# A hybrid mixer and expert layer: expert tables split ahead into fp16 halves in DRAM, three gathered blocks instead of two, 80 early score tiles

## Chip, core and metric

One of the eight cores of a Trainium2 chip runs the whole layer as one program. The metric is the device time of one execution in microseconds (us); less is better. The kernel before takes 4614.6 us (median of three runs, 4611.57 to 4617.51).

## What is computed

1024 latent tokens and 256 context tokens of 1024 features go through a parallel pair of token mixers (HGRN2 and gated linear attention, chunked scans with 12 heads in all), and then through a product-key expert layer (PEER) with 16,384 experts. The second half is what the change is mostly about:

```python
q = (tok @ wq).reshape(-1, PEER_HEADS, 2, PEER_SUB_DIM)      # 8 heads, two halves of 128
s1 = jnp.einsum("nhd,kd->nhk", q[:, :, 0], k1)               # 128 first keys
s2 = jnp.einsum("nhd,kd->nhk", q[:, :, 1], k2)               # 128 second keys
v1, i1 = lax.top_k(s1, 16)
v2, i2 = lax.top_k(s2, 16)
cand = (v1[..., :, None] + v2[..., None, :]).reshape(-1, 8, 256)
top_s, top_c = lax.top_k(cand, 16)
expert = take(i1, top_c // 16) * 128 + take(i2, top_c % 16)  # 128 experts per token
gate = jax.nn.softmax(top_s, axis=-1)
act = jax.nn.gelu(jnp.einsum("pd,ped->pe", xb, jnp.take(u, eb, axis=0)))
out = jnp.einsum("pe,ped->pd", gb * act, jnp.take(v, eb, axis=0))
```

The tables u and v have 16,384 rows of 1024 float32 numbers each (67 MB each).

## The kernel before

The work stands in four stages, one behind the other, each an `ExitStack` of pools in `tile_layer`.

**Heads.** For each head, 128-column slabs of the input projection are loaded (SP's DMA queue), split into two fp16 halves (`split`, L90: ScalarE makes the high half, VectorE the low half) and multiplied with the normalised tokens. Every product of two split operands is three matmuls (`mm3`, L95). `proj` (L299) makes one 128-column product for one range of tokens (24 matmuls), `v_natural` (L335) the value columns. Gates, scans, states and outputs of a head are computed while TensorE makes the projections of the next.

**Merge.** Merge gates, output projection, norm of the second sub-layer (`next_norm`, with `h2_rows`, which writes the normalised rows of the gathered tokens to DRAM), and the key choice of the first 512 tokens (`choosing`).

**Product keys and early scores.** `route` turns the top-16 lists of 128 tokens into key numbers and gates; `gate_block` makes the gate matrix of 32 tokens: one-hot rows `oh` on VectorE, matmuls `pgm` of a one-hot with a gated one-hot on TensorE, an eviction `gs` on ScalarE, and a store to `G_d`. Meanwhile `early_tile` makes scores of 128 experts for all tokens that go through every expert: `u_load`, `u_turn` (TensorE transposes `put`, two ScalarE copies, a GpSimd subtraction), `u_act` (matmuls `ph`, Gelu) and a store to `act_d`. How many early tiles stand between the steps of `prep` is set by a table of made-up durations that `prep` yields, against `U_US`.

**Groups of experts.** 32 groups of four expert tiles. Each tile's scores are either read back (`acr`) or made there (`ph`), multiplied by gates (`weigh`), and multiplied by the value rows (`v_tile`, `out_unit`, matmuls `pe`), whose sums VectorE adds to `acc`.

Blocks of 128 tokens come in two sorts. The first `NGB` = 2 blocks do not go through every expert: for each of their 128 slots GpSimd gathers one row of u per token by an indirect DMA, VectorE forms the dot product, and later one row of v per token is gathered and added to `gacc` (`gathering`, L864): 256 gathers of 512 KB per block. The others go through all 128 expert tiles. `gathers` puts two gathers behind every early tile, once both blocks are routed; `feed` spreads the rest over the groups in proportion to TensorE's work.

The program order of each engine and DMA queue is made by a scheduler at build time from the order in which the code records instructions; at run time each engine and each queue goes through its own list in order, and waits on semaphores.

## Time and profile before

| | |
|---|---|
| median of three runs | 4614.6 us (4611.57 to 4617.51) |
| span of the profiled execution | 4615.8 us |
| TensorE busy | 4416.1 us (96%) |
| VectorE busy | 2794.3 us (61%) |
| ScalarE busy | 1519.0 us (33%) |
| GpSimd busy | 1459.2 us (32%) |
| bytes moved by DMA | 709.58 MB, mean 154 GB/s |
| mean granted TensorE clock | 0.969 |

The profile is of one execution. Its span runs from the first to the last instruction, and it lies inside the spread of the three runs, so span and run time are taken as one number here. What one execution adds ahead of its first and behind its last instruction does not show in it. PE is TensorE (PEld its weight loads), DVE VectorE, ACT ScalarE, POOL GpSimd, SP the engine that issues most loads. A busy share is a mean over the four stages, which differ.

### The profile page before, as it was taken

The page shows a single profiled execution, that of the slowest core. Times are in us where ns is not written, and L with a number is a line of the kernel's source. Part 1 is how long each engine was busy: PE and PEld are TensorE (multiplying, and loading weights), DVE is VectorE, ACT ScalarE, POOL GpSimd, SP SyncE. Part 2 cuts the span into 40 slices and gives each one's busy share as a digit, 9 for nine tenths or more (in the row PEclk, how much of TensorE's full clock was granted, in tenths as well). Part 3 has the DMA queues.
Part 4 walks back from the last instruction along what each step waited for, and adds up shares of the span by engine and source line. Part 5 has one row for each costly group of instructions (what it writes and reads, how often), then busy time and mean ns, then how long its engine had stood idle before and what let it go on. Part 6 is the DMA issues. An engine that isn't in the chain of part 4 may idle for free.

```text
span 4615.8 us, 61540 instructions
## 1 busy us (share of the span) xinstructions
PE 4416.1 (96%) x24821; PEld 2509.4 (54%) x24821; DVE 2794.3 (61%) x4946; ACT 1519.0 (33%) x2251; POOL 1459.2 (32%) x1077
## 2 busy tenths in 40 slices
PE   7999999999999989899989999999999999999998
PEld 3666566566554444455555555555555555455554
DVE  5434544334564486656985443677777776877777
ACT  6333432322332222343334433322222222222222
POOL 2111111100110345523543111444444444444442
PEclk9999999999999999799998988999999999999999
DMA  4111111101147532224433435767777776777775
GB/s 165 37 33 38 42 38 33 46 27 43 42 121 231 193 117 78 84 100 148 137 130 131 149 140 178 235 230 264 253 255 251 236 253 230 256 252 258 246 248 199
DMA packets 421019, 709.58 MB, mean 154 GB/s; under 512 B 22031, under 2 KB 286714, under 8 KB 416638
## 3 DMA queue, kind: packets, MB, share of 16 engines
q1 hardware_dynamic: 219812, 291.35, 19.4%
q0 software_dynamic: 73728, 268.47, 17.7%
q10 hardware_dynamic: 127194, 145.83, 9.3%
q8 instruction: 195, 3.19, 0.3%
q14 instruction: 90, 0.74, 0.1%
HBM read 610.14 MB, written 95.43 MB: 153 GB/s over the span
## 4 chain that ended last, share of the span: by engine, by line
PE 71%; DVE 12%; ACT 6%; DMA 4%; issue 4%; POOL 3%; ACTq 0%; SPq 0%; DVEq 0%; POOLq 0%
PE pe L99 16%; PE ph L99 15%; PE pgm L1010 8%; ACT gs L1012 3%; PE pj_f0h L99 2%; PE pv_h L99 2%; PE pv_g L99 2%; PE pj_f1h L99 2%; PE pj_m L99 2%; PE pj_qh L99 2%; PE put L913 2%; PE pj_gh L99 1%; PE pq L99 1%; PE pso L99 1%; PE pj_kg L99 1%
## 5 line engine op out<-in xcount | busy, mean ns | idle before, releaser
L99 PE MATMUL ph<-hb,uT 128*128 128x256 f16 (+1 forms) x6144 | 1094.7, 335 | 5.1 <-ACT ac L933 2.6
L99 PE MATMUL pe<-v,w 128*128 128x512 f16 x4608 | 1013.0, 380 | 18.9 <-DVE acc L1102 13.3
L99 PEld LDWEIGHTS <-uT 128*128 128x128 f16 x6144 | 619.3, 101 | 409.4 <-issue 34.1
L99 PEld LDWEIGHTS <-w 128*128 128x128 f16 x4608 | 451.2, 98 | 567.3 <-issue 20.0
L920 POOL TENSOR_TENSOR uT<-uf,uT 128x512 f16<-128x512 f32 x256 | 361.0, 1420 | 476.1 <-ACT uf L919 474.2
L892 POOL DMA_INDIRECT row_False<-in_peer_u_dram,idx x256 | 303.2, 1185 | 459.1 <-DVE row_False L871 410.2
L892 POOL DMA_INDIRECT row_True<-in_peer_v_dram,idx x256 | 296.7, 1159 | 452.1 <-DVE gacc L876 406.3
L871 DVE SCALAR_TENSOR_TENSOR row_False<-row_False,h2n 128x1024 f32<-128x1024 f32 x256 | 345.0, 1354 | 139.0 <-DMA row_False<-in_peer_u_dram,idx 139.0
L1010 PE MATMUL pgm<-oh 128*128 128x128 f16 x1536 | 391.2, 410 | 37.9 <-ACT gs L1012 31.2
L876 DVE SCALAR_TENSOR_TENSOR gacc<-row_True,dots,gacc 128x1024 f32<-128x1024 f32 x254 | 356.2, 1402 | 1.6
L88 DVE TENSOR_TENSOR oh<-iota,rTr 128x1024 f16<-128x1024 f16 x192 | 151.8, 827 | 325.8 <-PE pgm L1010 325.8
L1012 ACT ACTIVATE gs<-pgm 128x512 f32<-128x512 f32 x192 | 204.8, 1067 | 419.0 <-PE pgm L1010 418.9
L1010 PEld LDWEIGHTS <-oh 128*128 128x128 f16 x1536 | 223.5, 146 | 179.0 <-issue 64.2
L933 ACT ACTIVATE ac<-ph 128x256 f32<-128x256 f32 (+1 forms) x256 | 125.3, 494 | 441.2 <-PE ph L99 434.1
L1102 DVE TENSOR_TENSOR acc<-pe,acc 128x512 f32<-128x512 f32 x372 | 252.9, 686 | 15.1 <-PE pe L99 15.0
L92 ACT ACTIVATE v<-vn 128x1024 f16<-128x1024 f32 x128 | 135.0, 1057 | 337.9 <-DMA vn<-in_peer_v_dram 222.5
L917 ACT ACTIVATE uT<-put 128x512 f16<-128x512 f32 x256 | 153.5, 600 | 272.3 <-PE put L913 264.2
L93 DVE SCALAR_TENSOR_TENSOR v<-vn,v 128x1024 f16<-128x1024 f32 x128 | 177.2, 1392 | 72.9 <-ACT v L92 68.5
L99 PE MATMUL pj_m<-hb,w_m 128*128 128x512 f16 x768 | 186.1, 399 | 2.2 <-DVE lf_g L85 1.6
L99 PE MATMUL pq<-hb,w_wq 128*128 128x512 f16 x768 | 180.7, 384 | 4.5 <-POOL w_wq L88 3.0
L99 PEld LDWEIGHTS <-hb 128*128 128x128 f16 x1536 | 150.3, 98 | 17.3
L919 ACT ACTIVATE uf<-put 128x512 f32<-128x512 f32 x256 | 154.9, 605 | 11.8 <-issue 7.6
(360 smaller groups left out, 5948.0 us busy)
## 6 DMA issues: line engine op xcount, KB each, us to landing
un<-in_peer_u_dram SPq DMA_DIRECT2D x128, 512.0 KB
vn<-in_peer_v_dram SPq DMA_DIRECT2D x128, 512.0 KB
G_d<-gs ACTq DMA_DIRECT2D x24, 2048.0 KB
gt<-G_d ACTq DMA_DIRECT2D x32, 1536.0 KB
act_d<-ac ACTq DMA_DIRECT2D x48, 384.0 KB
acr<-act_d SPq DMA_DIRECT2D x48, 384.0 KB
mw<-in_ada_w_dram SPq DMA_DIRECT2D x32, 512.0 KB
w_wq<-in_peer_wq_dram SPq DMA_DIRECT2D x32, 512.0 KB
```

Of the source, the lines that this page charges most:

```text
L88: eng.tensor_tensor(out=out, in0=in0, in1=in1, op=op)
L93: return V.scalar_tensor_tensor(out=lo, in0=src, scalar=float(scale), in1=hi, op0=ALU.mult, op1=ALU.subtract)
L99: PE.matmul(ps, lhsT=a(k), rhs=b(k), start=n == 0, stop=n == last)
L871: V.scalar_tensor_tensor(out=row, in0=row, scalar=1.0, in1=h2n, op0=ALU.mult, op1=ALU.mult, accum_out=dots[:, s:s + 1])
L876: V.scalar_tensor_tensor(out=gacc[n], in0=row, scalar=dots[:, s:s + 1], in1=gacc[n], op0=ALU.mult, op1=ALU.add)
L892: G.indirect_dma_start(out=row, out_offset=None, in_=src[0], in_offset=bass.IndirectOffsetOnAxis(ap=gsel[n][0][:, s:s + 1], axis=0))
L917: S.activation(hi, pv, AF.Copy, scale=SU)
L919: S.activation(uf, pv, AF.Copy, scale=SU)
L920: pace[0] = G.tensor_tensor(out=lo, in0=uf, in1=hi, op=ALU.subtract)
L1010: PE.matmul(pgm[:, t, :], lhsT=oh[:, 0, :, t1 + t], rhs=oh[:, j, :, t1 + t], start=j == 2, stop=j == 3)
L1012: S.activation(gs[:, :, q0:q0 + 4].rearrange("p i n -> p n i"), pgm, AF.Copy, scale=SA / SG)
L1102: vmark[0] = V.tensor_tensor(out=acc[n][:, hs], in0=ps, in1=acc[n][:, hs], op=ALU.add)
```

## The change

- During the heads, a generator `presplit` goes through both expert tables: 512 pieces of 128 rows x 512 columns are loaded (`pin`), split into fp16 halves (`pout`) and stored to `u_d` and `v_d`. `meanwhile` draws three pieces for each 512-column projection.
- `u_load` then reads the halves of u out of `u_d` by a transposing DMA, two of 256 KB for a tile; the TensorE transposes, the ScalarE copies and GpSimd's subtraction of `u_turn` go. `v_tile` reads ready halves from `v_d`; its split goes.
- The tables' rows are now grouped by first key, so a tile's 128 rows are neighbours, and `gate_block` swaps the roles of the keys.
- Three blocks (0, 1 and 4) are gathered, five go through every expert; `ph` is 256 and 384 columns wide instead of 256 and 512, and a group has 10 units of `pe` instead of 12.
- One-hot rows are made for 4 tokens at once instead of 8, so the token index, which is innermost, puts the 128 elements of a matmul operand 8 bytes apart instead of 16.
- 80 early tiles instead of 48; the made-up durations change, and `prep` routes the gathered blocks first. Row buffers of the gathers: 6 instead of 4; a gather's issue no longer stands behind `pace` (GpSimd's subtraction).

```diff
-TB = 8           # tokens whose one-hot rows are made at once
-NGB = 2          # blocks of 128 tokens whose experts' rows are gathered
-T0 = NGB * P     # the other tokens go through every expert
-TD = T - T0
+TB = 4
+GB = (0, 1, 4)
+DB = (2, 3, 5, 6, 7)
+TD = len(DB) * P
+DH = ((2, 4), (5, 8))
-U_US = 10.5
+U_US = 6.9
-AHEAD = 4
+AHEAD = 6
+PRE = 3.0
...
-    early = [e for e in range(NKEY) if e % GR == 0 or (e % GR == 2 and (e // GR) % 4 < NE2)]
+    early = [e for e in range(NKEY) if e * 5 % 8 < 5]
+    u_d = dram.tile([NKEY, 2, P, D], F16, name="u_d")
+    v_d = dram.tile([NKEY, P, 2, D], F16, name="v_d")
+    u_r = peer_u[0].rearrange("(e p) d -> e p d", p=NKEY)
+    v_r = peer_v[0].rearrange("(e p) d -> e p d", p=NKEY)
...
+        def presplit():
+            jobs = [(w, e, hf) for e in range(NKEY) for w in range(2) for hf in range(2)]
+            ins, outs = [], []
+            def load():
+                w, e, hf = jobs[len(ins)]
+                t = hs_.tile([P, HD], F32, name=f"pin{w}_{e}_{hf}", tag="pin", bufs=3)
+                ld(out=t, in_=(v_r if w else u_r)[e, :, hf * HD:(hf + 1) * HD])
+                ins.append(t)
+            def store():
+                w, e, hf = jobs[len(outs) - 1]
+                cs = slice(hf * HD, (hf + 1) * HD)
+                ld(out=v_d[e][:, :, cs] if w else u_d[e][:, :, cs].rearrange("a p d -> p a d"), in_=outs[-1])
+            load()
+            load()
+            for n, (w, e, hf) in enumerate(jobs):
+                if len(ins) < len(jobs):
+                    load()
+                o = hs_.tile([P, 2, HD], F16, name=f"pout{w}_{e}_{hf}", tag="pout", bufs=3)
+                split(ins[n], o[:, 0], o[:, 1], SV if w else SU)
+                if outs:
+                    store()
+                outs.append(o)
+                yield
+            store()
+        def meanwhile(w):
+            owed_[0] += PRE * w
+            while owed_[0] >= 1.0:
+                owed_[0] -= 1.0
+                next(ahead, None)
...
+            meanwhile(LEN[r] / HT)
...
-        for n in range(NGB):
+        for n in GB:
...
-                    with tc.issue_after(pace[0].ins):
-                        G.indirect_dma_start(out=row, out_offset=None, in_=src[0],
+                    G.indirect_dma_start(out=row, out_offset=None, in_=src[0],
...
-        un = pu.tile([P, D], F32, name=f"un{e}", tag="un", bufs=2)
-        ld(out=un, in_=u_r[:, e, :])
-        return un
+        uT = pu.tile([P, 2, KC, P], F16, name=f"uT{e}", tag="uT", bufs=3)
+        for j in range(2):
+            nc.sync.dma_start_transpose(out=uT[:, j], in_=u_d[e][j])
...
-                oh = pg.tile([P, 4, P, TB], F16, name=f"oh{n}_{c0}", tag="oh", bufs=2)
+                oh = pg.tile([P, 4, P, TB], F16, name=f"oh{n}_{c0}", tag="oh", bufs=4)
-                tt(V, oh[:, 0], iota, col(0), ALU.is_equal)
-                tt(V, oh[:, 1], iota, col(1), ALU.is_equal)
+                tt(V, oh[:, 0], iota, col(1), ALU.is_equal)
+                tt(V, oh[:, 1], iota, col(0), ALU.is_equal)
...
         def prep():
-            sel = route(NGB)
-            yield 9.0
-            yield from gating(range(NGB, 4), sel)
-            for n in range(NGB):
+            for n in (0, 1):
                 route(n)
-                yield 6.0
-            first = []
-            yield from choosing(1, ppg, lambda: first.append(route(4)))
-            yield from gating(range(4, 8), first[0])
+                yield 16.0
+            sel = route(2)
+            yield 16.0
+            yield from gating((2, 3), sel)
+            yield from choosing(1, ppg, lambda: route(4))
+            sel = route(5)
+            yield 16.0
+            yield from gating((5, 6, 7), sel)
...
-        vn = pd.tile([P, D], F32, name=f"vn{e}", tag="vn", bufs=2)
-        ld(out=vn, in_=v_r[:, e, :])
         v16 = pd.tile([P, 2, D], F16, name=f"v16_{e}", tag="v16", bufs=2 * GR)
-        vmark[0] = split(vn, v16[:, 0], v16[:, 1], SV)
+        ld(out=v16, in_=v_d[e])
```

Where instructions move, two places matter below. The first is the heads. This is SP's list of transfers around the loads of head 3 (`w_vh`, `w_gh`, `w_f0h`, `w_f1h` and `w_qh` are weight slabs of 512 KB), before:

```order
L340 DMA w_vh_1731<-in_w_in_dram 128x8x128
L340 DMA w_vh_1735<-in_w_in_dram 128x8x128
L168 DMA w_gh_2120<-in_w_in_dram 128x8x128
L168 DMA w_f0h_2319<-in_w_in_dram 128x8x128
L168 DMA w_f1h_2403<-in_w_in_dram 128x8x128
```

And the same queue in the changed kernel, between one weight slab of a head and the next (`pin` is a piece of a table that is loaded, `pout` its two halves that are stored):

```order
L175 DMA w_qh_3932<-in_w_in_dram 128x8x128
L317 DMA pin_32_1_3476<-in_peer_u_dram 128x512
L323 DMA v_d<-pout_31_0_3472 256x1x512
L317 DMA pin_32_0_3482<-in_peer_v_dram 128x512
L323 DMA v_d<-pout_31_1_3478 256x1x512
L317 DMA pin_32_1_3516<-in_peer_v_dram 128x512
L323 DMA u_d<-pout_32_0_3484 128x2x512
L317 DMA pin_33_0_3522<-in_peer_u_dram 128x512
L323 DMA u_d<-pout_32_1_3518 128x2x512
L317 DMA pin_33_1_3528<-in_peer_u_dram 128x512
L323 DMA v_d<-pout_32_0_3524 256x1x512
L390 DMA w_vh_4027<-in_w_in_dram 128x8x128
```

A weight slab that stood right behind the last one now stands behind some six loads and six stores of pieces (five of each are shown). On ScalarE, between two evictions of the projection `pj_f0h` of one head, before:

```order
L530 ACTIVATE at_f0h_2324<-pj_f0h_1_2351 128x512
L486 ACTIVATE ss_h_2182<-ss_h_2182 128x8
L530 ACTIVATE at_f0h_2324<-pj_f0h_2_2377 128x512
```

And in the changed kernel (`pout` from `pin` is the high half of a piece):

```order
L581 ACTIVATE at_f0h_2962<-pj_f0h_1_2995 128x512
L93 ACTIVATE pout_30_1_3292<-pin_30_1_3252 128x512
L430 ACTIVATE ke_h_1_3378<-lf_h_3311 128x1024
L432 ACTIVATE qe_h_1_3377<-lf_h_3311 128x1024
L536 ACT_TABLE_LOAD
L536 ACTIVATE ss_h_2820<-ss_h_2820,eps 128x8
L93 ACTIVATE pout_31_0_3298<-pin_31_0_3258 128x512
L93 ACTIVATE pout_31_1_3304<-pin_31_1_3290 128x512
L581 ACT_TABLE_LOAD
L581 ACTIVATE at_f0h_2962<-pj_f0h_2_3039 128x512
```

Three pieces now stand between two evictions; the next eviction cannot start before the piece ahead of it has landed. The second place is VectorE in the groups of experts, where `row` instructions use gathered rows and `acc` adds a sum from TensorE, before:

```order
L1102 TENSOR_TENSOR acc_22317<-pe_2_0_28692,acc_22317 128x512
L871 SCALAR_TENSOR_TENSOR row_2_False,dots_28521<-row_2_False,h2n_28519 128x1024
L1102 TENSOR_TENSOR acc_22317<-pe_2_1_28709,acc_22317 128x512
L871 SCALAR_TENSOR_TENSOR row_3_False,dots_28521<-row_3_False,h2n_28519 128x1024
L871 SCALAR_TENSOR_TENSOR row_5_False,dots_28521<-row_5_False,h2n_28519 128x1024
L1102 TENSOR_TENSOR acc_22318<-pe_3_0_28726,acc_22318 128x512
```

And in the changed kernel:

```order
L1142 TENSOR_TENSOR acc_26690<-pe_2_1_29054,acc_26690 128x512
L929 SCALAR_TENSOR_TENSOR row_37_False,dots_28376<-row_37_False,h2n_28374 128x1024
L929 SCALAR_TENSOR_TENSOR row_38_False,dots_28376<-row_38_False,h2n_28374 128x1024
L929 SCALAR_TENSOR_TENSOR row_39_False,dots_28376<-row_39_False,h2n_28374 128x1024
L929 SCALAR_TENSOR_TENSOR row_40_False,dots_28376<-row_40_False,h2n_28374 128x1024
L89 TENSOR_TENSOR acr_29199<-acr_29199,gt_29027 128x640
L89 TENSOR_TENSOR ac_29077<-ac_29077,gt_29027 128x640
L1125 TENSOR_TENSOR w_33_29139<-ac_29077,w_33_29139 128x640
```

More gathered rows stand between two sums, and no split of v. In the built order of the changed kernel 156 of the 768 uses of a gathered row stand ahead of the first `acc` and 612 behind it.

## Rows read from the trace of the kernel before

**Rows 1.** The page's part 1: busy us, share of the span, instructions.
```profile
PE 4416.1 (96%) x24821; PEld 2509.4 (54%) x24821; DVE 2794.3 (61%) x4946; ACT 1519.0 (33%) x2251; POOL 1459.2 (32%) x1077
```

**Rows 2.** Windows by stage: length, busy us by engine, granted clock, DMA share, GB/s.
```profile
70.00:1471.00 1401.00, 1355.80 (x9080) 848.61 (x9080) 637.02 (x1078) 493.87 (x711) 182.27 (x97) 0.98 0.19 55
1471.00:1887.00 416.00, 380.27 (x1768) 179.40 (x1768) 252.29 (x861) 112.93 (x154) 173.94 (x119) 0.96 0.43 137
1887.00:2890.00 1003.00, 942.53 (x4742) 568.81 (x4740) 606.79 (x1498) 395.07 (x566) 327.29 (x233) 0.91 0.38 136
2890.00:4616.00 1726.00, 1693.03 (x9080) 898.46 (x9080) 1272.98 (x1459) 477.73 (x760) 771.07 (x618) 0.99 0.74 244
```

**Rows 3.** The chain that ended last, in order of time: start us, us, what.
```profile
150.30 12.98 PE pj_f1h L99 x72
163.28 10.38 PE pj_qh L99 x48
...
3115.20 7.80 PE ph L99 x48
3123.00 15.54 PE pe L99 x72
```

**Rows 4.** Windows inside the heads: busy us by engine, clock, DMA share, GB/s.
```profile
300.00:1200.00 900.00, 877.94 (x5997) 558.29 (x5997) 377.48 (x661) 322.53 (x466) 117.36 (x60) 0.98 0.14 38
```

**Rows 5.** Windows in the last stage in which the DMA engines were full.
```profile
3085.00:3105.00 20.00, 20.00 (x110) 10.68 (x109) 15.47 (x22) 4.82 (x8) 10.05 (x8) 1.00 0.99 361
3130.00:3150.00 20.00, 20.00 (x110) 10.73 (x109) 15.39 (x20) 6.53 (x10) 10.45 (x8) 1.00 0.98 347
3180.00:3200.00 20.00, 20.00 (x110) 10.67 (x108) 16.77 (x20) 5.99 (x11) 8.84 (x7) 1.00 0.96 342
```

**Rows 6.** Groups by line in 2890 to 4616 us: count, busy us, mean ns, idle before.
```profile
L876 DVE SCALAR_TENSOR_TENSOR gacc<-row_True,dots,gacc 128x1024 f32<-128x1024 f32 x254 | 356.2, 1402 | 1.6
L892 POOL DMA_INDIRECT row_True<-in_peer_v_dram,idx x256 | 296.7, 1159 | 452.1 <-DVE gacc L876 406.3 <-DVE row_False L871 13.8 <-issue 12.1
L892 POOL DMA_INDIRECT row_False<-in_peer_u_dram,idx x202 | 239.5, 1186 | 392.8 <-DVE row_False L871 360.4 <-DVE gacc L876 8.0 <-issue 7.7
L92 ACT ACTIVATE v<-vn 128x1024 f16<-128x1024 f32 x122 | 128.7, 1056 | 329.9 <-DMA vn<-in_peer_v_dram 214.5 <-PE pe L99 106.6 <-PE put L913 8.4
L917 ACT ACTIVATE uT<-put 128x512 f16<-128x512 f32 x160 | 95.5, 597 | 267.6 <-PE put L913 259.5 <-PE pe L99 7.9
```

**Rows 7.** TensorE's timeline, gate matmuls and transposes: start us, us, operation, count.
```profile
2000.65 2.02 PE L1010 MATMUL pgm<-oh 128*128 128x128 f16 x8
2002.50 1.04 PE L99 MATMUL ph<-hb,uT 128*128 128x512 f16 x4
...
2012.47 0.60 PE L913 MATMUL put<-ident,un 128*128 128x128 f32 x4
...
2887.85 1.04 PE L913 MATMUL put<-ident,un 128*128 128x128 f32 x8
```

**Rows 8.** VectorE's timeline in the last stage: start us, us, operation.
```profile
3510.53 1.22 DVE L93 SCALAR_TENSOR_TENSOR v<-vn,v 128x1024 f16<-128x1024 f32 x1
...
3523.00 0.96 DVE L88 TENSOR_TENSOR acr<-acr,gt 128x768 f32<-128x768 f32 x1 [2.43 <-DMA acr<-act_d]
3523.88 0.95 DVE L88 TENSOR_TENSOR ac<-ac,gt 128x768 f32<-128x768 f32 x1
...
3527.80 0.68 DVE L1102 TENSOR_TENSOR acc<-pe,acc 128x512 f32<-128x512 f32 x1
3528.40 1.28 DVE L876 SCALAR_TENSOR_TENSOR gacc<-row_True,dots,gacc 128x1024 f32<-128x1024 f32 x1
3529.59 0.68 DVE L1102 TENSOR_TENSOR acc<-pe,acc 128x512 f32<-128x512 f32 x1
```

126 lines of the change are left out of this document (60 added, 66 removed).

## Prediction

> **What bounds the kernel now.** First the page's busy line: TensorE 96%, every other engine at or under 61% [rows 1]. That is a mean, so next the windows by stage [rows 2]: heads to 1471 us, merge to 1887, product keys with early scores to 2890, groups of experts to the end. TensorE is busy 1356 of 1401, 380 of 416, 943 of 1003 and 1693 of 1726 us. So each stage is TensorE's, and the stage table also shows who is next: in the groups VectorE has 1273 us of work and the DMA engines are 0.74 full at 244 GB/s; in the heads DMA is almost unused (0.19). The change takes from TensorE and gives to DMA and VectorE, so the question in each stage is which of the three ends last afterwards.
>
> The stretches of matmuls that follow each other in the chain give the prices [rows 3]: 48 `ph` matmuls (24 of 256 and 24 of 512 columns, one tile's scores) take 7.80 us, 72 `pe` of 512 columns 15.54, that is 0.216 each; 48 of a projection 10.38, so one `proj` of 512 columns 5.19.
>
> **Groups of experts (1726 us).** *TensorE:* 320 units of 12 `pe` instead of 384: 3840 x 0.216 = 829 us. Live tiles 48 instead of 80, each 640 columns instead of 768: 7.80 x 5/6 = 6.5 us, 312 us. The transposes go. Sum 1141.
>
> *VectorE:* 612 uses of a gathered row stand here in the changed order; now 458, the gathers that the two rows of POOL count [rows 6]. In the timeline an `acc` and a gather's use together take 3527.80 to 3529.59, of which 0.60 are the sum's and 1.19 the use's [rows 8]. 612 x 1.19 = 728; 320 sums x 0.60 = 192; gating and subtraction 0.88 each at 768 columns, so 128 x 2 x 0.88 x 5/6 = 188; the end some 30. Sum about 1140. The mean of 1402 ns in the group is more than 1.19 us [rows 6]; by it the uses cost 858 and the sum is 1270. The splits of v go (1.22 us each [rows 8]).
>
> *DMA:* a gather moves 128 x 1024 x 4 bytes = 0.524 MB. Now 458 x 0.524 + 80 tiles of u and 128 of v x 0.524 + 48 read-backs x 0.393 + 32 gate loads x 1.573 + ends 8 = 427 MB, against 244 x 1726 = 421 in the table [rows 2], so the account holds. After: 612 x 0.524 = 321; v 67; 48 transposing pairs 25; 80 read-backs x 0.328 = 26; 32 gate loads x 1.311 = 42; ends 8. Sum 490 MB in fewer us. In the three windows where DMA was full it moved 361, 347 and 342 GB/s [rows 5]: mean 350, so 490 MB take 1400 us. Bounds: 361 gives 1357; the stage's own 244/0.74 = 330 gives 1485.
>
> So DMA ends last here, ahead of TensorE by some 260 us. VectorE's list is in order, and a use of a row waits for its landing; behind it stand the sums that free `pe`'s PSUM tiles, so TensorE waits as well. With filling and end I take **1420**, a gain of 306. The six row buffers allow 6 x 1420/612 = 14 us between issue and use, enough, since 3.1 MB in flight are 9 us at 350 GB/s.
>
> **Product keys and early scores (1003 us).** TensorE before: 48 tiles x 7.8 = 374; gate matmuls, 8 in 1.85 us (2000.65 to the `ph` at 2002.50), 0.231 each [rows 7], x 1536 = 355; transposes, keys and the rest some 148; 877. So 126 us are gaps and stretches at the lower clock (granted 0.91 [rows 2]). After: 80 x 6.5 = 520; transposes of u gone, some 98 left; 1280 gate matmuls at a new price. A gate matmul has 128 columns and takes longer than a `pe` of 512 (0.216), so something in it costs; what sets it apart is that both operands' elements lie 16 bytes apart. They will lie 8 apart. Bounds: no better, 0.231; as the contiguous 128-column transposes, 0.11 (four `put` end after 0.60 us, eight after 1.04, so four more cost 0.44 [rows 7]). I take 0.12, half of 0.231, in proportion to the bytes that an operand spans, which is also near the contiguous row: 154 us, against 296. Sum 520 + 98 + 154 + the same 126 = **900**, with 1040 if the spacing buys nothing. Gain 103. VectorE, 607 busy now, gets some 100 more uses at 1.19: under 730, hidden below 900. GpSimd loses its subtractions.
>
> [...]
>
> The transposing loads occur nowhere in this trace. As ordinary traffic, a tile's 0.524 MB take 1.5 us at 350 GB/s, against 900/80 = 11 us per tile; two tiles are fetched ahead. I cost them at that; the bad end is a rival. [...]
>
> **Heads (1401 us).** Added: 512 pieces, each 0.262 MB in and 0.262 out: 268 MB. ScalarE: 512 x 0.597 (the 128 x 512 copy [rows 6]) = 306, with 494 now makes 800 of 1401. VectorE: half of 1.22 and a little, 0.65 x 512 = 333, with 637 now makes 970. Neither fills. DMA: three pieces per `proj` are 1.57 MB in 5.19 us, besides 38 GB/s of weights [rows 4], 0.2 MB. At 361 GB/s [rows 5] that is 4.9 us, just hidden; at the rate that the weights' traffic shows per share, 38/0.14 = 271, it is 6.5, and TensorE loses 1.3 us x 171 `proj` = 220. What waits then: ScalarE's list has three pieces between two evictions, the evictions free the two PSUM tiles of the projections; and on SP weight slabs stand behind piece stores that wait for VectorE. Near the good end, since 171 projections are 888 of the 1401 us and no pieces are drawn in the others, where DMA catches up, I take **+60**; ends 0 and 220. A sixth more VectorE work in front of the scans is in it.
>
> **Merge (416 us).** Eight more small transposes and stores beside 380 us of matmuls: 0.
>
> **Sum.** 4615.8 + 60 - 103 - 306 = **4267**. The span of 4615.8 is 1.2 us above the median, so the same number stands for the time. The runs differ by 0.13%; 0.2% is taken as the least that can be told from no change.
>
> **Rivals.**
> 1. *Forecast*, 4140 to 4390: chance 0.60.
> 2. *The heads pay the slow DMA rate*: 220 instead of 60, 4427. For it: the weights' 271 GB/s is the only rate that the heads themselves show [rows 4]; against: 342 to 361 in the groups [rows 5]. 0.11.
> 3. *The spacing buys nothing*: gate matmuls stay at 0.231, 142 us more, 4409. For it: no row shows another spacing; against: the only other 128-column rows are contiguous and twice as fast [rows 7]. 0.11.
> 4. *DMA does not bind in the groups*: at a lasting 420 GB/s the 490 MB take 1170 us; then VectorE and TensorE (1141) set about 1190, and the time is 4037. For it: DMA was never asked for more than in bursts; against: even full it moved 361 at most [rows 5]. 0.08.
> 5. *The transposing loads are slow*, the one that ends above before. TensorE takes one tile of early scores in 6.5 us and cannot start without it. At a tenth of 361 GB/s a tile takes 14.5 us: the keys' stage becomes 80 x 14.5 = 1160, and if the transfer holds the DMA engines in the groups too, these have 48 x 14.5 + (490 - 25)/0.35 = 2025 instead of 1420. Time 5130 (4530 if the engines stay free). It decides from 1.5 + 349/48 = 8.8 us per tile (60 GB/s) on: there the groups alone eat the gain of 349. [...] 0.10.
>
> **How the numbers follow.** The likeliest is case 1, 4267. Cases 2 and 3 widen the range upward to 4490 (both with a bad end of the groups), downward I go to 4090, part of the way to case 4; left out are most of case 4, case 5, together 0.17. Faster: cases 1 to 4 less a remainder, 0.88; slower: case 5 and a little, 0.11; same 0.01.
>
> **What will show it.** Heads: the stage's length, ScalarE's waits for `pin`, DMA share (0.19 + 268 MB/350 GB/s/1401 = 0.74 forecast). Keys: the pitch of eight gate matmuls (0.93 us expected, 1.85 if wrong), waits of `ph` for `uT`. Groups: GB/s near 345 and DMA share near 1 with TensorE at 0.80 busy, waits of VectorE for rows; if instead DMA has room and TensorE is full, case 4. A transposing load that lands after more than 8 us makes the prediction wrong, as would a new wait of SP's queue that holds back weights in the heads.

## The result: slower by 4.4%

| | before | changed | forecast |
|---|---|---|---|
| median of four runs, us | 4616.1 (4611.6 to 4622.3) | 4837.2 (4786.1 to 4869.2) | 4267 (4090 to 4490) |
| ratio, 95% interval | | 1.0437 (1.0383 to 1.0492) | |
| span of the profiled execution | 4615.8 | 4784.2 | |
| heads | 1401 | 1632 (+231) | +60 |
| merge | 416 | 422 (+6) | 0 |
| product keys and early scores | 1003 | 1068 (+65) | -103 |
| groups of experts | 1726 | 1592 (-134) | -306 |

The changed kernel is slower, outside the range, and by another sign than forecast. The stages are cut at the first merge matmul, the first `ph` and the first `pe`, in every kernel below. Their differences, 231 + 6 + 65 - 134 = 168, are the whole difference of the two profiled spans; three terms of the sum are off, by 171, 168 and 172 us. The profiled execution is the quickest of the four; the others took 43 to 83 us more, and no profile says in which stage. The slowest execution, 4869.2 us, is 1.7% above the quickest, counts as a slow run and is left out of the ratio, so differences of medians below go by the median of the other three, 4828.7.

**The profile after.** The page's busy line, which answers to [rows 1]:

```profile
PE 3910.2 (82%) x22778; PEld 2283.1 (48%) x22778; DVE 3095.4 (65%) x5908; ACT 1377.2 (29%) x2098; POOL 1417.7 (30%) x1077
```

TensorE is busy 506 us less, and the kernel takes longer: it now waits. In the chain that ended last, by engine, DMA stands where TensorE stood with 71%:

```profile
DMA 35%; PE 20%; DVE 18%; issue 13%; POOL 6%; ACT 6%; SPq 2%; ACTq 0%; DVEq 0%; POOLq 0%
```

The windows by stage, which answer to [rows 2] (length, busy us of TensorE, its weight loads, VectorE, ScalarE and GpSimd, granted clock, DMA share, GB/s):

```profile
70.00:1702.00 1632.00, 1413.42 (x9080) 877.89 (x9080) 984.36 (x1591) 790.30 (x1224) 183.16 (x97) 0.94 0.70 212
1702.00:2124.00 422.00, 381.56 (x1762) 179.35 (x1763) 249.77 (x848) 115.86 (x162) 173.53 (x118) 0.96 0.44 136
2124.00:3192.00 1068.00, 842.90 (x5786) 605.73 (x5785) 674.16 (x1938) 292.26 (x404) 331.19 (x241) 0.91 0.87 194
3192.00:4784.00 1592.00, 1227.49 (x6000) 606.00 (x5998) 1162.39 (x1482) 139.97 (x248) 725.67 (x612) 0.88 1.06 304
```

Read share and rate together. In the groups the engines of the DMA are full (1.06) at 304 GB/s; before, full windows moved 342 to 361 [rows 5]. In the keys' stage they are 0.87 full at 194 GB/s. Something takes DMA time without moving bytes. TensorE, busy 0.77 of the groups' stage where it was 0.98, is granted a clock of 0.88 there, where it was 0.99.

The waits of the heads (engine, line, for whom; us in total, times, longest):

```profile
DVE pout L94 <- ACT pout L93: 405.2, 309, 4.8
...
ACT pout L93 <- DMA u_d<-pout: 253.5, 174, 14.0
ACT pout L93 <- DMA v_d<-pout: 214.1, 158, 4.4
```

ScalarE stands still for 468 us because a piece's output buffer is still being stored, and VectorE behind it. I had said that waits for `pin`, the loads, would show; it is the stores. In the chain that ended last, landings of `u_d` and `v_d` stores make up 34% of the heads' stage. The waits of TensorE itself (the three longest):

```profile
PE kt_h L443 <- ACT kn_h L438: 49.4, 8, 8.5
PE py_g L644 <- ACT v_g L401: 16.5, 5, 5.4
PE pv_h L100 <- ACT v_h L401: 16.0, 9, 3.3
```

Added up over the heads, TensorE waits 170.5 us for ScalarE (22.8 before), 39.4 for VectorE (22.0) and 7.9 for GpSimd (none). That is 173 us more, and the other 58 of the 231 are TensorE's own: the same 9080 matmuls take 1413.42 us at a granted clock of 0.94, and 1355.80 at 0.98 before [rows 2]. The sign that the prediction named for SP's queue, weight slabs held back behind stores, does not show: waits for weight slabs come to 24 us, 26 before.

In the keys' stage TensorE waits for the transposing loads:

```profile
PEld L100 <- DMA uT<-u_d: 135.4, 21, 14.7
PE ph L100 <- DMA uT<-u_d: 127.7, 20, 14.2
```

and its timeline shows such a wait beside gate matmuls of the new spacing:

```profile
2235.34 0.60 PE L100 MATMUL ph<-hb,uT 128*128 128x256 f16 x2 [4.17 <-DMA uT<-u_d]
2250.19 2.74 PE L100 MATMUL ph<-hb,uT 128*128 128x256 f16 x12 [14.25 <-DMA uT<-u_d]
2252.73 1.13 PE L1052 MATMUL pgm<-oh 128*128 128x128 f16 x8
2253.67 1.16 PE L100 MATMUL ph<-hb,uT 128*128 128x256 f16 x6
```

Eight gate matmuls give way to the next after 2253.67 - 2252.73 = 0.94 us; at twice the spacing it was 1.85 [rows 7]. In the groups TensorE waits for VectorE's sums, and VectorE for gathered rows:

```profile
PE pe L100 <- DVE acc L1142: 292.2, 61, 14.7
...
DVE gacc L934 <- DMA row_True<-in_peer_v_dram,idx: 205.4, 123, 10.5
```

So there are two questions: what the transposing loads cost in the last two stages, and what in the pieces' way through ScalarE's list slows the heads. A scale for small differences: four kernels here have the very same heads (the changed one, e3, e5, e7), and they took 1632, 1636, 1642 and 1635 us. Keys and groups repeat less well where transposing loads are in them: 1031 to 1075 and 1579 to 1648 us in the changed kernel and the runs below that keep the transposing loads and alter the pieces.

### The profile page after: what moved, and what is told of

It is laid out like the page before. It is cut to its first block, busy times and chain, and to the rows that moved or that the text cites. A ratio compares the mean times of both kernels' runs of the same rounds, so it can differ in the third digit from the quotient of the medians.

```text
span 4784.2 us, 61229 instructions
## 1 busy us (share of the span) xinstructions
PE 3910.2 (82%) x22778; PEld 2283.1 (48%) x22778; DVE 3095.4 (65%) x5908; ACT 1377.2 (29%) x2098; POOL 1417.7 (30%) x1077
## 4 chain that ended last, share of the span: by engine, by line
DMA 35%; PE 20%; DVE 18%; issue 13%; POOL 6%; ACT 6%; SPq 2%; ACTq 0%; DVEq 0%; POOLq 0%
DMA row_True<-in_peer_v_dram,idx 10%; DMA u_d<-pout 6%; PE ph L100 6%; DMA v_d<-pout 5%; DMA uT<-u_d 4%; DMA row_False<-in_peer_u_dram,idx 4%; POOL row_False L949 3%; DMA gt<-G_d 3%; PE pgm L1052 3%; DVE pout L94 3%; DVE gacc L934 2%; ACT pout L93 2%; PE pj_m L100 2%; PE pq L100 2%; DVE row_False L929 2%
## 5 line engine op out<-in xcount | busy, mean ns | idle before, releaser
L100 PE MATMUL ph<-hb,uT 128*128 128x256 f16 (+1 forms) x6144 | 908.6, 306 | 134.9 <-DMA uT<-u_d 127.7
L949 POOL DMA_INDIRECT row_False<-in_peer_u_dram,idx x384 | 481.1, 1253 | 688.5 <-DVE row_False L929 579.2
L949 POOL DMA_INDIRECT row_True<-in_peer_v_dram,idx x384 | 444.3, 1157 | 689.7 <-DVE gacc L934 574.1
L94 DVE SCALAR_TENSOR_TENSOR pout<-pin,pout 128x512 f16<-128x512 f32 x512 | 372.0, 734 | 406.3 <-ACT pout L93 405.2
L934 DVE SCALAR_TENSOR_TENSOR gacc<-row_True,dots,gacc 128x1024 f32<-128x1024 f32 x381 | 488.1, 1281 | 213.1 <-DMA row_True<-in_peer_v_dram,idx 205.4
L929 DVE SCALAR_TENSOR_TENSOR row_False<-row_False,h2n 128x1024 f32<-128x1024 f32 x384 | 477.1, 1262 | 155.3 <-DMA row_False<-in_peer_u_dram,idx 149.3
L93 ACT ACTIVATE pout<-pin 128x512 f16<-128x512 f32 x512 | 319.5, 628 | 527.4 <-DMA u_d<-pout 253.5
L89 DVE TENSOR_TENSOR oh<-iota,rTr 128x512 f16<-128x512 f16 x320 | 131.1, 439 | 252.3 <-PE pgm L1052 219.1
L1052 PE MATMUL pgm<-oh 128*128 128x128 f16 x1280 | 178.2, 295 | 52.6 <-ACT gs L1053 28.0
L1052 PEld LDWEIGHTS <-oh 128*128 128x128 f16 x1280 | 146.1, 117 | 77.7 <-issue 56.1
```

The lines of the kernel that those rows point to most:

```text
L89: eng.tensor_tensor(out=out, in0=in0, in1=in1, op=op)
L93: S.activation(hi, src, AF.Copy, scale=float(scale))
L94: return V.scalar_tensor_tensor(out=lo, in0=src, scalar=float(scale), in1=hi, op0=ALU.mult, op1=ALU.subtract)
L100: PE.matmul(ps, lhsT=a(k), rhs=b(k), start=n == 0, stop=n == last)
L929: V.scalar_tensor_tensor(out=row, in0=row, scalar=1.0, in1=h2n, op0=ALU.mult, op1=ALU.mult, accum_out=dots[:, s:s + 1])
L934: V.scalar_tensor_tensor(out=gacc[n], in0=row, scalar=dots[:, s:s + 1], in1=gacc[n], op0=ALU.mult, op1=ALU.add)
```

## Experiments on the last two stages

**Splitting ahead left out (e2).** The other tiles are not split; every tile reads tile 0's halves.

```diff
-            jobs = [(w, e, hf) for e in range(NKEY) for w in range(2) for hf in range(2)]
+            jobs = [(w, e, hf) for e in range(1) for w in range(2) for hf in range(2)]
...
-            nc.sync.dma_start_transpose(out=uT[:, j], in_=u_d[e][j])
+            nc.sync.dma_start_transpose(out=uT[:, j], in_=u_d[0][j])
...
```

> The changed kernel with only the first 4 of the 512 pieces split during the heads; every expert tile then reads tile 0's halves, so the splitting of the other tiles is left out, and nothing else. Theory (the heads pay for the pieces, and nothing of them is left afterwards): the heads' stage goes back from 1632 us to about 1401, keys stay near 1069 and groups near 1599, so the time falls by about 231, to some 4560 to 4610, still about that of the kernel before. Rival (the pieces' stores also disturb what comes later, or the heads were slowed by the re-laid buffers): the heads stay above 1550, or the later stages shrink too.

The four executions took 4607.5, 4539.1, 4637.5 and 4638.0 us, the kernel before beside them 4623.0 (median). The heads' window:

```profile
70.00:1482.00 1412.00, 1355.43 (x9080) 848.43 (x9080) 639.24 (x1082) 495.26 (x714) 181.61 (x96) 0.98 0.19 57
```

1412 us, with the busy times of before to within 3 us: of the heads' loss of 231 us, 220 are the pieces'. Without that loss the rest of the change gains little: the quickest execution is 1.8% below the kernel before, the other three are within 16 us of it.

**TensorE turns u again (e3).** The transposing loads are undone, and with them go a buffer of `uT` (two for three) and one of `ph` (one for two).

```diff
-        for j in range(2):
-            nc.sync.dma_start_transpose(out=uT[:, j], in_=u_d[e][j])
+        un = pu.tile([P, D], F32, name=f"un{e}", tag="un", bufs=2)
+        ld(out=un, in_=u_r[e])
...
+        for q in range(2):
...
+            for k in range(4):
+                PE.transpose(pt[:, k * P:(k + 1) * P], un[:, (q * 4 + k) * P:(q * 4 + k + 1) * P], ident)
...
+            S.activation(hi, pv, AF.Copy, scale=SU)
...
+            S.activation(uf, pv, AF.Copy, scale=SU)
+            G.tensor_tensor(out=lo, in0=uf, in1=hi, op=ALU.subtract)
```

> The changed kernel with the transposing loads alone undone: u is read as plain fp32 rows (the same bytes per tile) and turned by TensorE, split by ScalarE and GpSimd as in the kernel before; splitting in the heads, three gathered blocks, spacing and v's halves stay. Theory A (the transposing loads cost three to four times their bytes in DMA time, 5 to 6.5 us of the 16 engines per tile): keys fall from 1069 to about 950 (80 tiles x 1.1 us of transposes come back to TensorE, the 128 us of waits for uT go), groups from 1599 to about 1400 to 1450, at 340 to 350 GB/s; in all 270 to 300 us less, about 4540. Theory B (the third gathered block fills the DMA engines whatever brings u in): keys gain some 50, groups stay within 40 us of 1599 at 305 GB/s; about 4750.

4559.1 us, ratio to before 0.986 (0.9842 to 0.9878): with this one part undone the change is a small gain, of 1.4%. Keys and groups:

```profile
2127.00:3162.00 1035.00, 900.25 (x6399) 669.22 (x6397) 763.29 (x1929) 455.50 (x737) 540.34 (x404) 0.95 0.57 200
3162.00:4560.00 1398.00, 1228.32 (x6400) 640.15 (x6400) 1235.83 (x1482) 232.45 (x428) 898.85 (x702) 0.95 0.94 346
```

The groups do what theory A says: the same bytes at 346 GB/s, 1398 us. The keys' stage does not (1035, not 950): the waits for `uT` go, but TensorE has 57 us of work more and waits 57.8 us for GpSimd's half of `uT`.

**The third gathered block undone (e5).**

```diff
-GB = (0, 1, 4)
-DB = (2, 3, 5, 6, 7)
+GB = (0, 1)
+DB = (2, 3, 4, 5, 6, 7)
...
-            yield from choosing(1, ppg, lambda: route(4))
-            sel = route(5)
-            yield 16.0
-            yield from gating((5, 6, 7), sel)
+            yield from choosing(1, ppg, lambda: first.append(route(4)))
+            yield from gating((4, 5, 6, 7), first[0])
```

> The changed kernel with the third gathered block alone undone: blocks 0 and 1 gather, block 4 goes through the gate matrix and the expert tiles again (768 columns). Theory A (transposing loads cost more, the third block as such is worth its price): without the block DMA has 134 MB less, but TensorE has 768 `pe` and 256 gate matmuls more: groups about 1500 to 1560 with TensorE above 0.9 busy, keys 1100 to 1140 as each tile is longer; total about 4750 to 4830, little gained. Theory B (the third block is what makes the change slower): groups fall to 1450 or less and the total to below 4700.

4701.3 us, ratio 1.0162 (1.0135 to 1.019). The groups:

```profile
3330.00:4698.00 1368.00, 1348.34 (x6768) 662.35 (x6768) 935.55 (x1162) 160.35 (x248) 409.85 (x356) 0.99 0.86 264
```

Neither expectation fits whole. The groups fall to 1368, as theory B says, with TensorE full; but the keys' stage grows to 1201 us, and the total stays above 4700. Transposing loads and the third block together overfill the DMA engines of the groups (share 1.06 in the changed kernel), and taking either away relieves them (0.94 in e3, 0.86 here). By medians, the one gives 270 us and the other 127.

**The same loads without the transposition (e7).** Bytes, place, queue and buffers stay; u is left unturned.

```diff
-            nc.sync.dma_start_transpose(out=uT[:, j], in_=u_d[e][j])
+            ld(out=uT[:, j].rearrange("p a b -> p (a b)"), in_=u_d[e][j])
```

> The changed kernel with each transposing load replaced by an ordinary load of the same bytes from the same place into the same buffer; u is thus left unturned, and nothing else changes. Theory A (the transposition costs, not the second reading of u): no waits of ph for uT in the keys, 1076 falls to some 940; in the groups the DMA engines come to 345 GB/s and 1592 falls to some 1400; total about 4460 (4420 to 4520), which would be the forecast's price for these loads with the heads' loss on top. Theory B (the loads' place in the queue, or that u is written to DRAM and read again): both stages stay within 50 us, total above 4680.

4422.0 us (4415.8 to 4429.7), ratio 0.9566 (0.9546 to 0.9586). Keys and groups:

```profile
2122.00:3052.00 930.00, 822.52 (x5788) 598.22 (x5786) 670.63 (x1944) 292.39 (x404) 336.83 (x241) 0.96 0.64 222
3052.00:4414.00 1362.00, 1169.98 (x6000) 594.10 (x6000) 1156.24 (x1483) 140.84 (x249) 752.80 (x612) 0.93 0.95 355
```

This settles it. The transposition costs 138 us in the keys and 230 in the groups of the profiled executions, 407 in the medians. In the keys TensorE's waits for DMA fall from 128 to 9 us. The groups move the same 483 MB in both kernels; the DMA view of the groups' stage, first of the changed kernel and then of this one, shows in what (q0 is the queue of the gathers, q1 that of SP's loads: packets, MB, and the time that the packets took as a share of the 16 engines'):

```profile
DMA packets 288194, 483.48 MB, mean 304 GB/s; under 512 B 104606, under 2 KB 181750, under 8 KB 288115
...
q0 software_dynamic: 88128, 320.90, 60.2%
q1 hardware_dynamic: 121197, 117.85, 33.5%
```

```profile
DMA packets 209821, 483.50 MB, mean 355 GB/s; under 512 B 15164, under 2 KB 92370, under 8 KB 209742
...
q0 software_dynamic: 88128, 320.90, 61.2%
q1 hardware_dynamic: 42764, 117.84, 22.7%
```

89,442 packets of less than 512 bytes stand in place of some 11,000 larger ones, an eighth as many. For the same 118 MB the packets of SP's loads take 0.335 x 1592 = 533 us of the 16 engines with the transposing loads among them, and 0.227 x 1362 = 309 without; the gathers' own packets take longer beside them as well, 958 us for 834. By the length of the stage a transposing tile costs 230/43 = 5.3 us more than an ordinary one (86 loads, 43 tiles, stand in this stage in either kernel). The three kernels with ordinary loads of u, e3, e7 and e6 below, have runs within 0.5% of each other; the changed one has 1.7%, and others with transposing loads have 0.5% (e5), 1.0% (e1) and 2.2% (e2).

**The transfers by themselves (e11, e14).** Not the layer: 64 tiles by transposing loads, then 64 by ordinary ones, then 64 transposing beside 256 row loads of 0.524 MB on ScalarE's queue.

```diff
+    for e in range(64):
+        last = tile_in("ta", e, True)
+    for e in range(64):
+        last = tile_in("pb", e, False)
+    for e in range(64):
+        tile_in("tc", e, True)
+    for i in range(256):
+        row = po.tile([P, D], F32, name=f"row{i}", tag="row", bufs=6)
...
+        st_(out=row, in_=u_r[i % NKEY])
```

> Not the layer but the transfers by themselves: 64 tiles by pairs of transposing loads with nothing beside them, then the same 64 tiles by ordinary loads, then 64 tiles by transposing loads beside 256 row loads of 0.524 MB on ScalarE's queue; the output is not the reference's. Theory A1 (the transposition is slow by itself): 4 to 6 us per tile in the first stretch, against 1.4 to 1.8 in the second. Theory A2 (it is quick by itself, 2.0 to 2.6 us per tile as the fastest tenth of its packets at 18 ns says, and slowed by the traffic beside it): 2.0 to 2.6 in the first stretch, 4 to 6.5 in the third. Theory A3 (its issue on SP sets the pace, 1.58 us per load in the changed kernel): 3.2 in the first stretch, and the row loads unhurt.

In this run the row loads did not wait and ran beside all three stretches, so it does not tell A1, A2 and A3 apart. It shows the mixture: row loads and transposing loads, row loads and ordinary ones, row loads and transposing ones (us, busy times of the idle engines, clock, DMA share, GB/s):

```profile
100.00:420.00 320.00, 0.00 (x0) 0.00 (x0) 0.00 (x0) 1.00 1.12 209
430.00:590.00 160.00, 0.00 (x0) 0.00 (x0) 0.00 (x0) 1.00 1.04 398
600.00:970.00 370.00, 0.00 (x0) 0.53 (x1) 0.00 (x0) 1.00 1.14 189
```

The DMA engines are full in all three, and with transposing loads they move half. In the next run the row loads were held back by a copy from the last ordinary tile.

> The transfers by themselves again, with the row loads now held back until the ordinary loads have landed (in the earlier run they ran beside all three stretches: transposing tiles then took 6 us each and both queues together moved 207 GB/s, ordinary tiles 2.7 us and 398 GB/s). Theory A1 (the transposition is slow by itself): 4 to 6 us per tile in the first stretch. Theory A2 (quick by itself, slowed by other traffic): 2.0 to 2.6 us there, 4 to 6.5 in the third stretch. Theory A3 (the issue on SP sets the pace when alone): 3.0 to 3.4 there. The ordinary loads alone: 1.4 to 1.6.

Transposing alone, ordinary alone, transposing beside row loads, and the row loads that were left (with the last copies of the output at its start):

```profile
100.00:220.00 120.00, 0.00 (x0) 0.00 (x0) 0.00 (x0) 1.00 1.04 191
235.00:325.00 90.00, 0.00 (x0) 0.00 (x0) 0.00 (x0) 1.00 0.96 321
345.00:670.00 325.00, 0.00 (x0) 0.27 (x1) 0.00 (x0) 1.00 1.13 199
700.00:930.00 230.00, 0.00 (x0) 0.00 (x0) 0.00 (x0) 1.00 1.03 411
```

Alone a tile of 0.524 MB takes 0.524/0.191 = 2.7 us transposing and 1.6 ordinary, both with three tile buffers, for which the ordinary loads waited 47.4 us. In the third stretch 116 transposing loads were issued in 325 us, 58 tiles, 5.6 us per tile. Beside them 64 row loads passed, and without the time that these take by themselves (64 x 0.524/0.411 = 82 us) it is 4.2 us per tile; 58 x 2.7 + 64 x 0.524/0.411 = 238 us would be the two kinds one behind the other, and together they took 325. A1 falls, and the price lies just above A2's 2.0 to 2.6: the theories of a cost by mixture and of one alone each hold a part. What of the 2.7 is the issue on SP is not told apart: 11 issues took 14.96 us, 1.36 each, but the DMA engines were full as well.

## Experiments on the heads

**More buffers, another queue (e1, e8).** e1 has `bufs=4` for `pout`, and a smaller descriptor space for the gathers (`dynamic_dma_scratch_size` 2048 instead of 4096), which its expectation does not mention; e8 issues the stores from ScalarE:

```diff
-                ld(out=v_d[e][:, :, cs] if w else u_d[e][:, :, cs].rearrange("a p d -> p a d"), in_=outs[-1])
+                st_(out=v_d[e][:, :, cs] if w else u_d[e][:, :, cs].rearrange("a p d -> p a d"), in_=outs[-1])
```

> The changed kernel with four output buffers for the pieces of the heads instead of three, all else alike. Theory H1 (each piece holds one of three buffers until its store has landed, 4 to 5 us after its issue, and ScalarE's in-order list stands still until then): a fourth buffer lets a third more pieces through in the same time, the 467 us of ScalarE's waits for stores shrink by more than half and the heads fall from 1632 to 1500 to 1560 us. Theory H2 (the DMA engines give the heads no more than some 236 GB/s whatever waits): within 20 us of 1632. Keys and groups unchanged under both.

> The changed kernel with the pieces' stores issued on ScalarE's DMA queue instead of SP's, same bytes, same buffers. Theory H3 (a store stands behind the pieces' own loads in SP's queue, and its landing comes late for that): the stores land sooner, ScalarE's waits for them halve, the heads fall by 50 to 120 us to 1510 to 1580, although ScalarE has 512 issues more. Theory H2 (bandwidth of the 16 engines): no gain; 1620 to 1750, the issues on ScalarE added.

Heads 1640 us with four output buffers, 1663 with the other queue; ratios to before 1.0395 (1.0344 to 1.0446) and 1.0502 (1.0443 to 1.056). H1 in its simple form and H3 fall. But in e1 ScalarE's waits only changed their object, from the stores to the loads, and TensorE waits 168.8 us for ScalarE as it did (170.5):

```profile
ACT pout L93 <- DMA pin<-in_peer_v_dram: 222.7, 151, 13.5
ACT pout L93 <- DMA pin<-in_peer_u_dram: 193.8, 137, 5.0
```

**Transfers left out, in whole or in part (e9, e10, e15).** All splits stay in all three. e9 leaves out the loads after the third piece and the stores after the fourth, e15 the loads alone, e10 the low halves' stores; every tile reads tile 0's halves.

```diff
...
+                if len(ins) < 3:
+                    ld(out=t, in_=(v_r if w else u_r)[e, :, hf * HD:(hf + 1) * HD])
...
+                if len(outs) > 4:
+                    return
```

(The second part stands in e9 alone. In e10 it is instead:)

```diff
+                if len(outs) > 4:
+                    ld(out=v_d[e][:, 0, cs] if w else u_d[e][0, :, cs], in_=outs[-1][:, 0])
+                    return
```

> The changed kernel with the pieces' splitting left in on ScalarE and VectorE (512 pieces, same sizes, same places in their lists), but all their loads after the third and all their stores after the fourth left out; every tile then reads tile 0's halves. Theory (what the heads lose is the pieces' transfers, by whichever mechanism): heads 1420 to 1470 instead of 1632. Rival H4 (692 us more work on two in-order lists, ahead of evictions and scans, is itself the loss): heads above 1560.

> The changed kernel with only the high half of each piece stored (the store of the low half is left out, a quarter of the pieces' bytes; every tile then reads tile 0's halves); loads, buffers, issues and splits as they were. Theory H2 (in the stretches with projections the DMA engines are the limit, some 250 to 270 GB/s at 0.8 to 0.9 of their time): a quarter fewer bytes takes a third to two thirds of the heads' loss of 231 us away: 1480 to 1560. Theory H1b (load and store round trips over three buffers each, whatever the bytes): the heads stay above 1600, for the number of trips is the same.

> The changed kernel with the pieces' loads left out after the third, their splits and all their stores left in (the pieces hold the same values again and again; every tile reads tile 0's halves). Under H1b (either round trip alone can hold ScalarE's list, as the moved wait says): the heads stay near 1600 to 1635 although half the bytes are gone. If it takes both trips, or the bytes: 1500 to 1560, between the 1475 without transfers and the 1632 with all.

The heads of e9, e10 and e15:

```profile
70.00:1545.00 1475.00, 1376.45 (x9081) 862.03 (x9082) 959.99 (x1591) 771.69 (x1223) 188.10 (x97) 0.96 0.18 54
```

```profile
70.00:1696.00 1626.00, 1414.57 (x9081) 882.44 (x9082) 986.25 (x1590) 787.62 (x1222) 178.32 (x96) 0.94 0.56 172
```

```profile
70.00:1597.00 1527.00, 1390.03 (x9081) 865.80 (x9081) 984.11 (x1590) 783.22 (x1223) 187.03 (x97) 0.95 0.43 139
```

Without transfers 74 of the 231 us stay: that is the price of 512 more instructions in each of two in-order lists (5 us above what I had expected at most); TensorE waits 72.0 us for ScalarE there, 22.8 before. A quarter fewer bytes give back 6 us, within the scatter, although the DMA share falls from 0.70 to 0.56, which speaks against the rate of the DMA engines. With stores but no loads 126 us are lost: the stores make up 52 of the other 157, and the rest comes with the loads; loads without stores were not run.

**Four buffers of both kinds (e13), GpSimd in ScalarE's place (e16, e17).** e13 and e17 have `bufs=4` for `pin` and `pout`, load three pieces ahead instead of two, and have a descriptor space of 1024; only their heads are read. e16 and e17 make the high half on GpSimd:

```diff
-                split(ins[n], o[:, 0], o[:, 1], SV if w else SU)
+                tsc(G, o[:, 0], ins[n], SV if w else SU, ALU.mult)
+                V.scalar_tensor_tensor(out=o[:, 1], in0=ins[n], scalar=SV if w else SU, in1=o[:, 0], op0=ALU.mult, op1=ALU.subtract)
```

> The changed kernel with four input and four output buffers for the pieces instead of three and three, and loads issued three pieces ahead instead of two. With four output buffers alone ScalarE's waits only moved from the stores' landing to the loads' (417 us), and the heads stayed at 1640. Theory H1b (round trips of both kinds over three buffers each): with both at four the heads fall to 1500 to 1570, towards the 1475 that are left without any transfers. Theory H5 (depth is not it: the order of SP's list, or bursts at the limit of the DMA engines): the heads stay above 1610. The gathers' descriptor space is smaller here, so only the heads are read.

> The changed kernel with the high half of each piece made by GpSimd instead of ScalarE, all else alike (512 pieces, both halves, same loads, stores and buffers). Theory (what costs in the heads is that ScalarE's in-order list stands still at a piece whose transfer is late, with the evictions of the projections behind it): ScalarE never waits for a piece, and the heads fall from 1632 to 1460 to 1540. Rival (VectorE's list, which also has every piece in it, or TensorE's other waits, hold just as long): 1600 or more. Only the heads are read.

> The same with four input and four output buffers instead of three, and loads three pieces ahead. If waits for transfers are still what costs once ScalarE is out of them, the heads come another 20 to 40 us lower than with three, as they did with ScalarE in (1632 to 1600); if they are then no longer waited for, both are within 10 us of each other. The gathers' descriptor space is smaller, so only the heads are read.

The heads of e13, e16 and e17:

```profile
70.00:1670.00 1600.00, 1411.82 (x9080) 881.25 (x9080) 990.29 (x1592) 787.68 (x1225) 181.21 (x97) 0.94 0.69 216
```

```profile
70.00:1908.00 1838.00, 1422.32 (x9080) 884.47 (x9080) 1066.29 (x1591) 496.67 (x712) 1020.73 (x609) 0.88 0.63 188
```

```profile
70.00:1798.00 1728.00, 1416.90 (x9082) 879.81 (x9083) 1100.79 (x1591) 495.10 (x712) 1029.02 (x609) 0.91 0.65 200
```

e13 lies between its theories: the fourth buffer gives 32 us, more than the scatter and less than expected. In e16 the heads are longer, against my theory, although no piece is left in ScalarE's list: GpSimd takes 1.49 us (median) for what ScalarE did in 0.63, and now VectorE waits for it and TensorE for VectorE:

```profile
DVE pout L332 <- POOL pout L84: 539.6, 378, 4.8
...
PE sc_h L450 <- DVE scT L451: 193.7, 16, 40.7
```

Added up, TensorE's waits for ScalarE fall from 170.5 to 75.6 us, and those for VectorE rise from 39.4 to 333.2. So e16 does not clear ScalarE's list, which was the road in the changed kernel; it opens another. With four buffers (e17) these heads are 110 us shorter. The waits reach TensorE through whichever list holds both pieces and work that TensorE waits for. What holds that list, as far as shown, is a piece that waits for a buffer, until a store has landed or, with four output buffers, a load. How much of the 157 us more than the 32 deeper buffers would give back stays open; more than four were not tried.

## The parts that held, put together

**Four tokens' rows alone (e4)**, in the kernel before (the made-up duration of a step is halved with it, so the early tiles stand where they stood):

```diff
-TB = 8
+TB = 4
...
-                oh = pg.tile([P, 4, P, TB], F16, name=f"oh{n}_{c0}", tag="oh", bufs=2)
+                oh = pg.tile([P, 4, P, TB], F16, name=f"oh{n}_{c0}", tag="oh", bufs=4)
```

> The kernel before with one part of the change alone: one-hot rows for four tokens at once instead of eight (four buffers instead of two, so the same memory). Theory (8-byte spacing of the operands' elements halves a gate matmul, 0.255 to 0.139 us on the mean of its group in the two traces): 1536 x 0.09 to 0.116 = 140 to 178 us less TensorE work in the keys' stage, of which most shows: 4440 to 4500, the other stages unchanged. Rival (twice as many VectorE instructions of half the size take the gain back, or the gate matmuls were hidden behind VectorE): less than 50 us, above 4565.

4442.5 us, ratio 0.9609 (0.9593 to 0.9625): one constant is worth 3.9%. The keys' stage, 1003 before:

```profile
1886.00:2725.00 839.00, 751.80 (x4851) 516.41 (x4852) 658.45 (x1896) 407.10 (x587) 351.43 (x244) 0.97 0.47 167
```

**Three gathered blocks, 80 early tiles, nothing split ahead (e6); three gathers per early tile in place of two (e12).** e6 is e3 with the generator empty (`ahead = iter(())`) and v loaded and split when used; e12 adds:

```diff
-G_E = 2
+G_E = 3
```

> The parts of the change that held, without those that did not: one-hot rows for four tokens, three gathered blocks, 80 early tiles with contiguous rows; u is turned by TensorE and v split when it is used, nothing is split during the heads. From the stages of other runs: heads 1401, merge 416, keys 1035 as with TensorE turning u, groups TensorE 1228 busy, DMA 483 MB at 346 GB/s = 1398, VectorE 1236 + 128 x 1.22 = 1392 busy; I expect about 1450 there and 4370 in all (4310 to 4440), faster than both kernels. Rival (VectorE's in-order list becomes the bound of the groups, with waits for rows in it): groups 1550 or more, 4470, no better than the kernel before with four tokens' rows alone.

> The faster kernel of the earlier run (three gathered blocks, four tokens' rows, TensorE turns u, no splitting ahead) with three gathers per early tile in the keys' stage instead of two. Theory (in the groups the DMA engines, 0.95 full, and VectorE, 1360 of 1422 us, end last, and in the keys' stage both have room, 0.57 and 765 of 1032): some 75 gathers move, 39 MB and 100 us of VectorE; groups 1320 to 1350, keys 1035 to 1070, total 4270 to 4310 against 4349. Rival (the keys' stage lengthens by what the groups save, since VectorE's in-order list holds the one-hot rows behind the uses): 4330 or more.

e6: 4348.7 us, ratio 0.9395 (0.9372 to 0.9418). e12: 4302.2 us, ratio 0.9304 (0.9289 to 0.932), the quickest version found. The groups of e6, then keys and groups of e12:

```profile
2928.00:4350.00 1422.00, 1238.97 (x6400) 638.39 (x6398) 1360.14 (x1610) 362.88 (x554) 1004.06 (x702) 0.96 0.95 342
```

```profile
1893.00:2959.00 1066.00, 912.27 (x6397) 675.59 (x6394) 884.82 (x2001) 457.57 (x737) 627.42 (x482) 0.95 0.65 230
2959.00:4300.00 1341.00, 1216.10 (x6400) 639.39 (x6400) 1261.12 (x1532) 351.01 (x554) 880.95 (x624) 0.96 0.93 332
```

Moving 78 gathers (702 less 624 of GpSimd's instructions) from a stage whose VectorE and DMA are full (in e6 1360 of 1422 us and a share of 0.95) into one that has room for them (765 of 1032 us and 0.57) shortens the first by 81 us and lengthens the other by 34.

## Why the prediction was wrong, by its steps

**What bounds the kernel, the merge, the sum's form.** Right: the stages are independent, their terms add up, and the merge moved by 6 us.

**Gate matmuls, 0.231 to 0.12 us.** Right: 0.94 us for eight, 0.118 each (by their group's busy time, 178.2 us for 1280, it is 0.139, and before 391.2 for 1536, 0.255). In e4 the keys' stage fell by 164 us; by the forecast's prices it is 1536 x (0.231 - 0.12) = 170. Rival 3 is out. 8 bytes apart, the gate matmul costs 0.118 us, near the 0.11 of the contiguous 128-column transposes [rows 7]; that the price goes with the bytes that an operand spans was an estimate, which two spacings do not show.

**Transposing loads "as ordinary traffic", 1.5 us per tile.** This step failed, and undoing it turns the sign: e7, with the heads' loss still in it, is 4.3% quicker than the kernel before, while undoing the heads' loss instead (e2) brings about the time of before. The rest of the two stages' working was close: with ordinary loads in that place the keys take 930 us (forecast 900) and the groups 1362 (forecast 1420, at 350 GB/s; measured 355). A transposing tile costs 2.7 us alone and 5.6 beside row loads: in e14 these loads moved 191 GB/s alone, where ordinary ones moved 321, and 93 in the mixture (30.2 MB in 325 us). Rival 5 had the right mechanism: its formula for the groups, 48 tiles plus 465 MB at 350 GB/s, gives 48 x 5.6 + 1329 = 1598 us, and 1592 were measured. That close a fit is luck: row loads passed in those 5.6 us too, and with the 4.2 that are left without them the formula gives 1530; in the stage itself a tile costs 5.3 us more than an ordinary one. Its point of decision, 8.8 us per tile, was too high, because it set the loss against the whole forecast gain and left the keys out; with the heads 171 and the keys 168 us short, either price was enough. I gave it 0.10. An operation that no row shows deserved more than that.

**Heads, +60 with ends of 0 and 220.** This term failed by size and by mechanism. Both ends were worked out from bytes and DMA rates; the measured 231 lies near the bad end and rival 2's 220, but by luck, for bytes are not what costs: a quarter fewer gave back 6 us. The share of the DMA engines came out as said, 0.70 for 0.74. The pieces cost 74 us as instructions in two in-order lists, and 157 more with their transfers: a piece holds one of three buffers of each kind through its load, its splits and its store, and ScalarE's list stands behind it. The prediction named what waits ("ScalarE's list has three pieces between two evictions"), and then priced it by bandwidth. That three buffers explain the whole 157 is not shown, since a fourth gave back 32. And the sum has no term for the clock: 58 of the 231 us are the same matmuls at 0.94 instead of 0.98. The argument that DMA catches up outside the projections was not tested.

**Groups, 1420 at DMA's limit.** Right but for the transposing loads: its terms came out (483 MB moved, 490 forecast; VectorE busy 1162 us, 1140 forecast), and in e3, e6 and e7 the DMA engines are 0.94 to 0.95 full, with TensorE busy 1170 to 1239 us of 1362 to 1422 and its longest waits those for VectorE's sums. Rival 4 is out: full, the DMA engines moved 304 to 355 GB/s in this stage. Row loads by themselves reached 411 in e14, near the 420 that it asked for, but the stage's own mixture did not.

**The range** left out case 5 as a whole. With case 5 at its due it would have had to reach above 4800.

## What to carry to other kernels

A transfer that transposes was not priced by its bytes here: 0.524 MB took 2.7 us alone, where ordinary loads took 1.6, and 5.6 beside row loads (e14). Before such a transfer replaces work of another engine in a stage whose DMA will be full, time it alone and beside that stage's own traffic. Work threaded into idle places of another stage can cost by standing in in-order lists and by keeping buffers, even where no engine and no DMA is full: here 231 us in the heads, with TensorE 0.87 busy and a DMA share of 0.70; 74 of them stayed without the transfers (e9), and a fourth buffer of each kind gave back 32 (e13). And take a change of many parts one part at a time: here one constant gained 3.9%, the parts that held together 6% (7% with one more gather per early tile), and the whole lost 4.4%.

## What the hardware showed that was not expected

- Transposing loads and row loads slowed each other in e14: 191 GB/s alone and 411 for row loads alone, but 199 together, with the DMA engines full in each stretch (shares 1.04, 1.03 and 1.13).
- Ordinary loads of 2 KB rows from the fp16 halves ran at 321 GB/s by themselves (with three tile buffers) and 4 KB rows at 411; the two kinds together at 398.
- The time of the changed kernel scatters by 1.7% over four runs, and by 0.3% with ordinary loads of the same bytes; of the other kernels with transposing loads one scatters by 2.2% and one by only 0.5%.
- GpSimd took 1.49 us (median) to scale and cast a piece of 128 x 512 that ScalarE did in 0.63.
